# Start addresses of the SBUF buffers modulo 256 bytes in a two-layer hybrid network

## The chip, the core and the metric

The kernel runs on one core of a Trainium2 chip. The metric is the device time of one execution in microseconds, median of three runs. The core's engines appear in the profile as PE (TensorE, matrix products; PEld is its weight load), DVE (VectorE), ACT (ScalarE), POOL (GpSimd) and SP (SyncE, which only issues transfers). SBUF is the on-chip memory from which TensorE reads both operands of a product, PSUM the memory into which it writes. A product has a stationary operand (the weights, 128 by 128) and a moving one (128 rows, here 128 to 512 columns).

## The reference

Two layers over 1024 latent tokens, with 256 context tokens beside them, model width 1024. Layer 0 mixes tokens by a chunked gMLP, layer 1 by windowed attention; each is followed by a convolutional gated FFN (hidden width 2816).

```
h = modulate(rms_norm(x, norm_g[i, 0]), sh1, sc1)
layer 0:  y = chunk_mlp(h, ...)          # z = gelu(h @ w_in); u, v = split(z); v = layer_norm(v)
                                         # s = w_s (128 x 128 per group) applied to v; y = (u * s) @ w_out
layer 1:  y = window_attention(h, hc, ...)   # |q - k| <= 128 plus all context keys plus a sink
x = x + g1 * rms_norm(y, norm_g[i, 1])
h = modulate(rms_norm(x, norm_g[i, 2]), sh2, sc2)
x = x + g2 * rms_norm(conv_ffn(h, ...), norm_g[i, 3])
# conv_ffn: a, b = split(h @ w_up); a = width-3 depthwise conv of a + conv_b; (gelu(a) * b) @ w_down
```

sh, sc and g come from silu(c) @ ada_w + ada_b. All of it is float32. The context tokens go through layer 0 whole and serve layer 1 as keys and values only.

## The kernel before, in words

Each float32 operand is split into two float32r tiles, a rounded "hi" (a CAST on ACT) and a remainder "lo" (a subtraction on DVE). A product is three matmuls: hi with hi, hi with lo, lo with hi (`mm3`; two in the attention). Names in the profile read out<-moving,stationary: in the up-projection (`psB<-cmb,wh`) the inputs move and the weights stand, in the down-projection (`psA<-wh,ah`), the gMLP (`wh,big`, `wh,act`) and qkv the weights move and the activations stand.

Buffers are rings of tiles with one tag. In the pool `sb`, for the whole kernel: raw (3, float32 weights as loaded), row (10, general), wh and wl (4 each, split weights), gate, sm. In pools by stage, opened one after another at the same place by `open_pool` (mix, up0, down0, mix2, up1, down1): tmp (8), big (8, split inputs of the mixers), act (6), y, acc; in the up stages the 28 cmb tiles; in the down stages ah and al. Tiles of one ring stand one behind the other, so the address of a tile modulo 256 follows from the size of a tile and from what was laid out ahead of the ring.

Stages in order: gMLP of latent tiles 0 to 4, gMLP of latent tiles 5 to 7 and the context; 22 context jobs of the up-projection of layer 0 (256 columns, `up_ctx`); up0 (`up`, 22 jobs); down0 with the context's; qkv; attention, with its output projection (`wh,oc`) set between; up1; down1.

The up-projection (`lat_ffn`) uses seven products instead of eight, with sums of the inputs made once: `combine(g)` loads a half of 512 tokens (g = 0 or 1) from xT, the transposed input in DRAM, forms a11, a12, a22, s1, s2, s3, s4 of it and writes each, split, into its cmb tile, into the columns from g * 256. A cmb tile holds two k rows (k = 0, 1). One full job f is 7 products by 4 k by 3 = 84 matmuls of 512 columns (`up`). In layer 1, where g = 1 is late (its tokens come last out of the attention), the first five f run as plain jobs (`up_plain`) on g = 0 alone, without the seven-product scheme, 256 or 258 columns; they read the first 256 columns of both k rows of a11, a12, a22 and the row tiles A21. Their other half is made by five later half jobs ("g1", 256 columns). a11 and a12 have two extra columns in front (`off`), which in layer 1 hold the tokens of the neighbouring half.

The order on each engine comes from the tile scheduler, which works on the order of the program and on the waits between tiles. It finds them from the byte ranges that instructions touch in a tile. Some instructions are held in program order (`pins`, `keep_in_program_order`): the whole prologue on four engines, and a few norms.

Of the kernel before, what the change touches and what calls it, by code (L numbers as in the profile page):

```python
# [10 lines left out]
F32 = mybir.dt.float32  # L11
F32R = mybir.dt.float32r
AF = mybir.ActivationFunctionType
ALU = mybir.AluOpType

P = 128
D = 1024
KD = D // P
# [3 lines left out]
FFN = 2816  # L22
NF = FFN // P
# [9 lines left out]
def hybrid_kernel(  # L33
# [27 lines left out]
    sb = ctx.enter_context(tc.tile_pool(name="sb", bufs=1))  # L61
    stage_pool = {}

    def open_pool(name):
        if stage_pool:
            stage_pool.pop("guard").__exit__(None, None, None)
        stage_pool["guard"] = tc.tile_pool(name=name, bufs=1, reuse_waits="tile")
        stage_pool["pool"] = stage_pool["guard"].__enter__()

# [6 lines left out]
    def nm(s):  # L76
        uid[0] += 1
        return f"{s}_{uid[0]}"

    def t_raw():  # L80
        return sb.tile([P, 1024], F32, name=nm("raw"), tag="raw", bufs=3)

    def t_row(dt=F32, shape=(P, 1024)):
        return sb.tile(list(shape), dt, name=nm("row"), tag="row", bufs=10)

    def t_tmp(shape=(P, 648), dt=F32):
        return stage_pool["pool"].tile(list(shape), dt, name=nm("tmp"), tag="tmp", bufs=8)

    def t_big(shape, dt=F32R):
        return stage_pool["pool"].tile(list(shape), dt, name=nm("big"), tag="big", bufs=8)  # L90

    def t_act(shape=(P, 2, 644), dt=F32R):
        return stage_pool["pool"].tile(list(shape), dt, name=nm("act"), tag="act", bufs=6)

    def t_y(shape=(P, 5, 1024), dt=F32):
        return stage_pool["pool"].tile(list(shape), dt, name=nm("y"), tag="y", bufs=1)

    def t_acc():
# [5 lines left out]
    def t_sm(w=2):  # L104
        return sb.tile([P, w], F32, name=nm("sm"), tag="sm", bufs=24)

    def t_w(tag, dt=F32R, shape=(P, 1024)):
        return sb.tile(list(shape), dt, name=nm(tag), tag=tag, bufs=4)

    def psA(shape=(P, 2, 512)):  # L110
        return ps.tile(list(shape), F32, name=nm("psA"), tag="psA", bufs=2)
# [12 lines left out]
    def w_cols(w, col):  # L124
        return wsplit(w[:, col:col + P].rearrange("(k p) n -> p k n", p=P), KD)
# [27 lines left out]
    ident = const.tile([P, P], F32, name="ident")  # L153
    make_identity(nc, ident)
    ones_r = const.tile([P, P], F32R, name="ones")
    ones_f = t_tmp((P, P))
    G.memset(ones_f, 1.0)
    S.copy(ones_r, ones_f)
    ones = ones_r.bitcast(F32)
# [13 lines left out]
    def mod_cols(l, m, s):  # L173
        if (l, m) not in slots:
            slots[(l, m)] = len(slots)
        return modc[:, slots[(l, m)], s, :]
# [76 lines left out]
    def step(gen, n=1):  # L253
        for _ in range(n):
            next(gen, None)
# [51 lines left out]

    def hk(hb, z, k):
        if (z, k // 2) not in hb:
            hb[z, k // 2] = t_big((P, 2, 648))  # L310
        return hb[z, k // 2][:, k % 2, :]

    def build(hb, stage, l, mi, segs, zeros, W):
# [12 lines left out]
        for k in range(KD):  # L326
# [8 lines left out]
            S.copy(hk(hb, 0, k)[:, 0:W], tm[:, 0:W])  # L335
            V.tensor_sub(hk(hb, 1, k)[:, 0:W], tm[:, 0:W], hk(hb, 0, k)[:, 0:W])
            yield

    def halo(hb, xt, l, mi, c, col):
        tm = t_sm(KD)  # L340
        V.tensor_tensor(out=tm, in0=xt[:, :, c], in1=mod_cols(l, mi + 1, 0), op=ALU.mult)
        V.tensor_tensor(out=tm, in0=tm, in1=mod_cols(l, mi, 0), op=ALU.add)
        for q in range(KD // 2):
            V.tensor_copy(hb[0, q][:, :, col], tm[:, 2 * q:2 * q + 2])
            V.tensor_sub(hb[1, q][:, :, col], tm[:, 2 * q:2 * q + 2], hb[0, q][:, :, col])

    def up_cols(p, w, hb, c0, hw, halves=(0, 1)):
        wh, wl = w
# [80 lines left out]
    def lazy_y():  # L429
        box = []  # L430

        def y():
            if not box:
                box.append(t_y())
            return box[0]

        return y
# [281 lines left out]
    cols = {}  # L719
# [159 lines left out]
        group(3, finisher(0, tiles, y, gate, order, on_flip, mod, own), pre_last(),  # L879
              (lambda: s_part(14, True), lambda: s_part(15, True)), own)  # L880

    def ffn(l, stage, hb, W, nb, tiles, joff, gate, extra, pre_last, n_extra=1):
        hw, nbh = W // 2, 1 if nb <= 512 else 2
        bw = nb // nbh
        halves = tuple(range(nbh))
        order = list(range(len(tiles)))
        y = lazy_y()
        groups = [4, 4, 4, 4, 6]
        pend = []
        f = 0  # L890
        cw = cols["cw", l]

        def ab(f, fi, acts):
            wa = w_cols(w_up[l], f * P)
            pa = psA()
            up_cols(pa, wa, hb, 0, hw)
            wb = w_cols(w_up[l], FFN + f * P)
            pb = psA()
            up_cols(pb, wb, hb, 2, bw, halves)
            a = t_tmp()  # L900
            S.copy(a[:, 0:W].rearrange("p (a b) -> p a b", a=2), pa[:, :, 0:hw])
            cv = t_tmp()
            c = cv[:, 0:nb]
            G.tensor_scalar(out=c, in0=a[:, 2:2 + nb], scalar1=cw[:, NF + f:NF + f + 1],
                            scalar2=cols["cb", l][:, f:f + 1], op0=ALU.mult, op1=ALU.add)
            V.scalar_tensor_tensor(out=c, in0=a[:, 1:1 + nb], scalar=cw[:, f:f + 1], in1=c,
                                   op0=ALU.mult, op1=ALU.add)
            V.scalar_tensor_tensor(out=c, in0=a[:, 3:3 + nb], scalar=cw[:, 2 * NF + f:2 * NF + f + 1], in1=c,
                                   op0=ALU.mult, op1=ALU.add)
            S.activation(c, c, AF.Gelu_apprx_tanh)  # L910
            c2 = c.rearrange("p (a b) -> p a b", a=nbh)
            V.tensor_tensor(out=c2, in0=pb[:, 0:nbh, 0:bw], in1=c2, op=ALU.mult)
            if fi % 2 == 0:
                acts.append((t_act(), t_act()))
            ah, al = acts[-1]
            S.copy(ah[:, fi % 2, 0:nb], c)
            V.tensor_sub(al[:, fi % 2, 0:nb], c, ah[:, fi % 2, 0:nb])

        for gi, gn in enumerate(groups):
            acts, f0 = [], f  # L920
            for fi in range(gn):
                ab(f, fi, acts)
                f += 1
                step(extra, n_extra)
                if fi == 0 and pend:
                    pend.pop()()
            if gi < len(groups) - 1:
                pend.append(lambda f0=f0, gn=gn, acts=acts, gi=gi:
                            down_group(w_down[l], f0, gn, acts, joff, y, gi == 0, order))
        down_group(w_down[l], f0, gn, acts, joff, y, False, order,  # L930
                   finisher(stage, tiles, y, gate, order), pre_last())

    COMBOS = ("a11", "s2", "s1", "s3", "a12", "a22", "s4")

    def split_into(dst, src):
# [43 lines left out]
    def lat_ffn(l, stage, n0, halos, gate, between, steady, ctx=None, after=None):  # L979
# [2 lines left out]
        cb = cols["cb", l]  # L982
        open_pool("up%d" % l)
        pool = stage_pool["pool"]
        off = {n: 2 if n in ("a11", "a12") else 0 for n in COMBOS}
        HL = {}
        for n in COMBOS:
            for c in range(2):
                HL[n, c] = [pool.tile([P, 2, 512 + off[n]], F32R, name=nm("cmb"), tag="cmb%d_%d%s%d" % (l, z, n, c),
                                      bufs=1) for z in range(2)]  # L990
        keep = pool.tile([P, NF], F32, name=nm("keep"), tag="keep", bufs=1)

        def t_s():
# [87 lines left out]
        def up_ctx(f, nxt, fill):  # L1081
            W, more = next_weights(nxt)
            banks = [psB() for _ in range(2)]
            for bank, names in zip(banks, (("b11", "b21"), ("b12", "b22"))):
                for q in range(2):
                    for k in range(4):
                        wh, wl = (W[names[q]][z][:, k, :] for z in range(2))
                        mm3(bank[:, 0:CTX], wh, wl, cx[0, q][:, k, :], cx[1, q][:, k, :],
                            q == 0 and k == 0, q == 1 and k == 3)
                if bank is banks[0]:  # L1090
                    a = t_row(shape=(P, 1028))
                    for e in (0, 1 + CTX):
                        G.memset(a[:, e:e + 1], 0.0)
                    S.copy(a[:, 1:1 + CTX], bank[:, 0:CTX])
                step(more)
                step(fill)
            step(more, 9)
            conv_gate(f, a, CTX, banks[1][:, 0:CTX], SEQ)

        def up_plain(f, nxt, fill):  # L1100
# [3 lines left out]
            for pair_, half in ((("b11", "b21"), X), (("b12", "b22"), Y)):  # L1104
# [14 lines left out]
                    step(fill)  # L1119
                    step(more)  # L1120
                if half is X:
                    a = t_row(shape=(P, 1028))
                    G.memset(a[:, 0:1], 0.0)
                    S.copy(a[:, 1:257], X[:, 2:258])
                    S.copy(a[:, 513:514], X[:, 1:2])
                    S.copy(a[:, 257:513], X2[:, 0:256])
                    G.tensor_copy(keep[:, f:f + 1], a[:, 512:513])
# [3 lines left out]
        def up(f, groups, nxt):  # L1131
# [39 lines left out]
            product(Y, "s3", "t3", False)  # L1171
            S.copy(b2, wide(Y[:, 0:n]))
            product(X, "a12", "b21", False)
            a = t_row(shape=(P, 1028))
            av = halves(a[:, 1:1 + N])
            S.copy(av[:, :, 0, :], wide(X[:, 0:n]))
            if groups[0] == 0:
# [240 lines left out]
         flushes(True), first_weights, on_ctx, order=(3, 4, 0, 1, 2), mod=(0, 3))  # L1418

    def mix_pool():  # L1420
        open_pool("mix2")
        hold["h"] = {}
        return build(hold["h"], 2, 1, 0, [(0, 0, 640)], [], 640)

# [451 lines left out]
```

## Time and profile before

| | |
|---|---|
| median of 3 runs | 2947.26 us (2941.18 to 2949.09) |
| profiled execution, span from first to last instruction | 2937.7 us |
| instructions | 40168, of which 14834 matmuls |

The profiled execution's span lies 9.6 us below the median of the runs; sums below are made against the span.

The page lists per engine the busy time, its share of the span and the number of instructions, and the granted clock in tenths in 40 equal slices (PEclk, 9 is full). A row of the chain of waits has start, length and the work; a row of the timeline start, length of the group, engine, operands, shape of weights and moving tile, count. Durations of matmuls overlap, since a matmul's end includes the way through the array; the distance between two starts is what a matmul costs in a stream. Stages in the timeline: gMLP to about 830 us, context jobs 835 to 920, up0 to 1354, down0 to 1582, context down to 1690, qkv 1725 to 1835, attention to 2200, up1 2240 to 2685, down1 to 2938.

### The profile page before, as it was taken

The numbers are of one execution on the slowest core, as the hardware profiler recorded it, in microseconds if no ns is written. First come the engines' busy times: TensorE is split into PE (matmuls) and PEld (weight loads), VectorE is DVE, ScalarE is ACT, GpSimd is POOL, SyncE is SP. The second block draws the span as 40 slices with busy tenths as digits, with TensorE's granted clock in tenths as the row PEclk, the third lists the DMA queues.
The fourth block names the chain that finished last, engine by engine and source line by source line (L and its number), as shares of the span: only waits on it lengthen the run. The fifth ranks groups of instructions, "written<-read, shape, count | busy, mean of one in ns | idle before, by whom it ended". The sixth has DMA issues, their size and how long they took to land. (4 is left out here: it accounts for less than half of the span.)

```text
span 2937.7 us, 40168 instructions
## 1 busy us (share of the span) xinstructions
PE 2829.4 (96%) x14834; PEld 2404.4 (82%) x14834; DVE 2034.1 (69%) x3066; ACT 1353.6 (46%) x2279; POOL 678.1 (23%) x1003
## 2 busy tenths in 40 slices
PE   7999999999999999999999999899998999999999
PEld 5899988899898888888877777888887888888887
DVE  6557674756787888778643769897877877776333
ACT  4332242322575444543324534777775444444221
POOL 1151130720201212220003025564551211220000
PEclk9999999999999999999999999999999999999999
DMA  7764356532675333546844865356666233325532
GB/s 260 243 186 143 117 184 205 168 96 72 198 226 169 108 103 112 165 151 218 290 163 170 283 212 176 111 191 215 196 234 201 98 112 109 92 83 193 177 115 101
DMA packets 402310, 488.08 MB, mean 166 GB/s; under 512 B 17473, under 2 KB 296897, under 8 KB 402113
## 3 DMA queue, kind: packets, MB, share of 16 engines
q1 hardware_dynamic: 345697, 422.32, 44.7%
q10 hardware_dynamic: 55264, 58.99, 5.9%
q0 software_dynamic: 1152, 4.19, 0.4%
q8 instruction: 117, 1.92, 0.3%
q14 instruction: 80, 0.66, 0.1%
HBM read 388.96 MB, written 96.47 MB: 165 GB/s over the span
## 5 line engine op out<-in xcount | busy, mean ns | idle before, releaser
L50 PE MATMUL psB<-cmb,wh 128*128 128x512 f32 (+2 forms) x2584 | 756.5, 377 | 6.6 <-ACT s L50 3.2
L50 ACT CAST wh<-raw 128x1024 fp32r<-128x1024 f32 (+1 forms) x388 | 345.8, 904 | 510.5 <-PE psB L50 208.0
L50 PEld LDWEIGHTS psB<-cmb,wh 128*128 128x128 f32 x2584 | 471.5, 188 | 104.8 <-ACT row L50 4.4
L50 DVE TENSOR_TENSOR wl<-raw,wh 128x1024 fp32r<-128x1024 f32 (+1 forms) x388 | 399.1, 1040 | 131.4 <-ACT wh L50 130.6
L50 PE MATMUL psB<-cmb,wl 128*128 128x512 f32 (+2 forms) x1292 | 486.9, 377 | 0.0
L50 PE MATMUL psB<-wh,big 128*128 128x512 f32 x864 | 288.4, 402 | 2.7 <-DVE row L50 1.4
L50 PEld LDWEIGHTS psB<-cmb,wl 128*128 128x128 f32 x1292 | 243.1, 188 | 48.2
L50 POOL TENSOR_SCALAR sm<-sm 128x1 f32<-128x1 f32 (+1 forms) x76 | 41.4, 545 | 867.4 <-ACT tmp L50 317.2
L50 POOL TENSOR_TENSOR row<-raw,raw 128x512 f32<-128x512 f32 x44 | 72.5, 1647 | 606.4 <-DMA raw<-in_f_w_up_dram 489.4
L50 DVE TENSOR_TENSOR al<-raw,ah 128x1024 fp32r<-128x1024 f32 x74 | 90.5, 1224 | 167.8 <-ACT ah L50 167.6
L50 PE MATMUL psB<-wh,act 128*128 128x512 f32 x640 | 202.9, 395 | 1.6 <-DVE tmp L50 1.6
L50 PEld LDWEIGHTS psB<-wh,big 128*128 128x128 f32 x864 | 163.9, 191 | 42.4 <-ACT big L50 2.4
L50 PE MATMUL psA<-big,wh 128*128 128x320 f32 x1024 | 193.3, 310 | 2.6 <-ACT wh L50 1.4
L50 DVE SCALAR_TENSOR_TENSOR row<-row,cwcols,row 128x1024 f32<-128x1024 f32 (+2 forms) x142 | 160.5, 1130 | 37.9 <-ACT row L50 17.3
L50 ACT CAST ah<-raw 128x1024 fp32r<-128x1024 f32 x74 | 77.4, 1047 | 222.0 <-PE psB L50 150.6
L50 ACT CAST wh<-row 128x512 fp32r<-128x512 f32 (+1 forms) x132 | 100.7, 765 | 168.8 <-DVE row L50 77.4
L50 PE MATMUL psB<-wl,big 128*128 128x512 f32 x432 | 168.3, 399 | 0.0
L50 PEld LDWEIGHTS psA<-big,wh 128*128 128x128 f32 x1024 | 159.7, 188 | 3.6 <-ACT wh L50 2.0
L50 POOL TENSOR_SCALAR row<-row,sm,sm 128x128 f32<-128x128 f32 x160 | 120.5, 768 | 149.1 <-DMA row<-vscr 143.3
L50 PEld LDWEIGHTS psB<-wh,act 128*128 128x128 f32 x640 | 120.1, 188 | 30.1 <-issue 1.0
L50 PE MATMUL psB<-row,wh 128*128 128x256 f32 x744 | 137.1, 286 | 4.8 <-ACT wh L50 2.1
L50 DVE SCALAR_TENSOR_TENSOR acc<-raw,ccols,acc 128x1024 f32<-128x1024 f32 x63 | 79.7, 1287 | 87.1 <-DMA raw<-in_ada_w_dram 86.9
(264 smaller groups left out, 6285.6 us busy)
## 6 DMA issues: line engine op xcount, KB each, us to landing
raw<-in_f_w_up_dram SPq DMA_DIRECT2D x142, 512.0 KB, 4.4
raw<-actd SPq DMA_DIRECT2D x83, 512.0 KB, 4.3
raw<-in_a_w_in_dram SPq DMA_DIRECT2D x64, 512.0 KB, 4.6
raw<-in_ada_w_dram SPq DMA_DIRECT2D x64, 512.0 KB, 4.8
wh<-woscr SPq DMA_DIRECT2D x48, 512.0 KB, 4.3
raw<-in_f_w_down_dram SPq DMA_DIRECT2D x88, 256.0 KB, 4.0
actd<-row SPq DMA_DIRECT2D x39, 512.0 KB, 2.6
raw<-in_a_w_out_dram SPq DMA_DIRECT2D x35, 512.0 KB, 3.5
```

What stands on the lines that cost most here:

```text
L50: ins = fn(*a, **kw)
```

## The change

The pitch of every ring that TensorE reads becomes a multiple of 256 bytes, and small "lead" tiles set where a ring begins. The table gives the start modulo 256 of the tiles, as they are laid out in the two programs.

| tiles | before | after |
|---|---|---|
| raw (and oc, same ring) | 192 | 192 |
| wh, wl | 192 | 0 (lead of 16 floats) |
| row | 192, 224, 0, 32 ... (pitch 4128) | 192 (pitch 4352) |
| tmp | steps of 32 (pitch 2592) | 0 |
| big | 0, 64, 128, 192 (pitch 5184) | 0 in mix, 192 in mix2 |
| act | steps of 32 (pitch 5152) | 0 in mix, 192 in mix2 |
| cmb, first operand column | a11 0 to 96, s1 s2 s3 128, a12 128 to 224, a22 s4 0, k = 1 of a11 and a12 8 further | 0; in layer 1 the k = 1 rows of a11 and a12 at 16 |
| ah, al | 0 | 0 |

What is called distance below is the start of the stationary tile of the next matmul minus that of the moving tile of the current one, modulo 256. After the change it is, in steps between matmuls of 512 columns: 7231 times 0, 1152 times 192 (qkv, attention's output projection), 204 times 240 (steps into k = 1 of a11 and a12, layer 1). With 256 columns: 2270 times 64 (context jobs, attention), 598 times 0 (half jobs and some plain ones), 120 times 240. With 320 columns (first gMLP): 1535 times 0.

A cmb tile was [P, 2, n]; it is now a flat [P, lead + 2 pitch], of which the code takes a view with k as a dimension. In layer 0 a11 and a12 have no extra columns any more. ones_f becomes a tile of the row ring instead of tmp. Functions `halo` and `ffn`, which nothing calls, are gone.

```diff
+    leads = {"w": 16}
+    def sb_lead(tag):
+        n = leads.pop(tag, 0)
+        if n:
+            G.memset(sb.tile([P, n], F32, name=nm("lead"), tag="lead" + tag, bufs=1), 0.0)
...
+    def t_edged(n):
+        return sb.tile([P, 1088], F32, name=nm("row"), tag="row", bufs=10)[:, 0:n]
...
-    def t_tmp(shape=(P, 648), dt=F32):
+    def t_tmp(shape=(P, 640), dt=F32):
...
     def t_big(shape, dt=F32R):
+        lead("big")
...
-    def t_act(shape=(P, 2, 644), dt=F32R):
+    def t_act(shape=(P, 2, 640), dt=F32R):
+        lead("act")
...
     def t_w(tag, dt=F32R, shape=(P, 1024)):
+        sb_lead("w")
...
-    ones_f = t_tmp((P, P))
+    ones_f = t_row(shape=(P, P))
...
-            hb[z, k // 2] = t_big((P, 2, 648))
+            hb[z, k // 2] = t_big((P, 2, 640))
...
-        off = {n: 2 if n in ("a11", "a12") else 0 for n in COMBOS}
+        off = {n: 2 if n0 and n in ("a11", "a12") else 0 for n in COMBOS}
         HL = {}
+        home = 0
         for n in COMBOS:
+            pitch = 512 + 2 * off[n]
             for c in range(2):
-                HL[n, c] = [pool.tile([P, 2, 512 + off[n]], F32R, name=nm("cmb"), tag="cmb%d_%d%s%d" % (l, z, n, c),
-                                      bufs=1) for z in range(2)]
+                HL[n, c] = []
+                for z in range(2):
+                    lead_ = (-home - 4 * off[n]) % 256 // 4
+                    t = pool.tile([P, lead_ + 2 * pitch], F32R, name=nm("cmb"), tag="cmb%d_%d%s%d" % (l, z, n, c),
+                                  bufs=1)
+                    home += -(-4 * (lead_ + 2 * pitch) // 32) * 32
+                    HL[n, c].append(t[:, lead_:].rearrange("p (k n) -> p k n", k=2))
...
-            a = t_row(shape=(P, 1028))
+            a = t_edged(1028)
...
-        open_pool("mix2")
+        open_pool("mix2", big=48, y=16)
```

The order of instructions moves at two places. SP's queue begins before the change with the load of a_w_s (w_s of the gMLP):

```order
L50 DMA row_733<-in_a_w_s_dram 128x8x128
L50 DMA tmp_84<-in_c_dram 8x128
L50 DMA tmp_84<-in_c_ctx_dram 8x128
L50 DMA act_112<-in_ada_w_dram 128x4x128 x2
L50 DMA act_115<-in_ada_w_dram 128x4x128 x2
```

After the change that load stands behind the prologue's loads of w_in (raw):

```order
L50 DMA raw_412<-in_a_w_in_dram 128x2x512
L50 DMA raw_484<-in_a_w_in_dram 128x2x512
L50 DMA raw_561<-in_a_w_in_dram 128x2x512
L50 DMA row_735<-in_a_w_s_dram 128x8x128
L50 DMA row_737<-in_a_b_s_dram 128x1024
```

It moved 27 places back; the rest of the queue keeps its order there.

The second place is on PE in the plain jobs of layer 1, about 2240 us, where the last transposes out of the attention (`psA<-ident,row`) stand between the products. cmb_20599 to cmb_20602 are a11 (hi and lo, c = 0 and 1), row_20629 is A21, psB_21103 and psB_21104 the banks of the second plain job. Before, its products follow k by k, both banks in turn:

```order
L50 MATMUL psA_20923<-ident,row_20867 128x128 x7
L50 MATMUL psB_21103<-cmb_20601,wl_21002 128x258
L50 MATMUL psB_21104<-row_20629,wh_21001 128x256 x2
L50 MATMUL psB_21104<-row_20629,wl_21002 128x256
L50 MATMUL psB_21103<-cmb_20601,wh_21001 128x258
L50 MATMUL psB_21103<-cmb_20602,wh_21001 128x258
L50 MATMUL psB_21103<-cmb_20601,wl_21002 128x258
```

After the change (numbers are six higher: psB_21110 is the second bank of that job) only the products of the bank that reads A21 and the like stand there; the first products of other jobs follow, and then the k = 1 product of the first job's psA_20974 with cmb_20605 (a11, hi, c = 0), with a wait for ACT that has no counterpart before (it is for the cast by which combine(1) writes that tile):

```order
L50 MATMUL psA_21111<-row_20634,wl_21040 128x256
L50 MATMUL psB_21244<-cmb_20605,wh_21143 128x258 [waits PE_49,Activation_49]
L50 MATMUL psB_21244<-cmb_20606,wh_21143 128x258
L50 MATMUL psB_21244<-cmb_20605,wl_21144 128x258
L50 MATMUL psB_21245<-row_20634,wh_21143 128x256 [waits Activation_49]
L50 MATMUL psB_21245<-row_20634,wh_21143 128x256
L50 MATMUL psB_21245<-row_20634,wl_21144 128x256
L50 MATMUL psB_21245<-row_20634,wh_21143 128x256 x2
L50 MATMUL psA_20974<-cmb_20605,wh_20968 128x256 [waits Activation_49]
```

176 matmuls change their places around there, and with them neighbours on ACT, DVE, SP and POOL; elsewhere PE's order is that of before. Between the last transposes and the last row above stand 33 matmuls.

More of the change, by code (lines that the diff above doesn't have):

```diff
@@ L62, in hybrid_kernel, with open_pool @@
     stage_pool = {}
-    def open_pool(name):
+    def open_pool(name, **leads):
         if stage_pool:
             stage_pool.pop("guard").__exit__(None, None, None)
+        stage_pool["leads"] = leads
         stage_pool["guard"] = tc.tile_pool(name=name, bufs=1, reuse_waits="tile")
@@ L81, in t_raw, with lead @@
         return sb.tile([P, 1024], F32, name=nm("raw"), tag="raw", bufs=3)
+    leads = {"w": 16}
[3 more added lines that the diff above has]
+            G.memset(sb.tile([P, n], F32, name=nm("lead"), tag="lead" + tag, bufs=1), 0.0)
     def t_row(dt=F32, shape=(P, 1024)):
         return sb.tile(list(shape), dt, name=nm("row"), tag="row", bufs=10)
-    def t_tmp(shape=(P, 648), dt=F32):
+    def t_edged(n):
+        return sb.tile([P, 1088], F32, name=nm("row"), tag="row", bufs=10)[:, 0:n]
+    def lead(tag):
+        n = stage_pool["leads"].pop(tag, 0)
+        if n:
+            G.memset(stage_pool["pool"].tile([P, n], F32, name=nm("lead"), tag="lead" + tag, bufs=1), 0.0)
+    def t_tmp(shape=(P, 640), dt=F32):
         return stage_pool["pool"].tile(list(shape), dt, name=nm("tmp"), tag="tmp", bufs=8)
     def t_big(shape, dt=F32R):
+        lead("big")
         return stage_pool["pool"].tile(list(shape), dt, name=nm("big"), tag="big", bufs=8)
-    def t_act(shape=(P, 2, 644), dt=F32R):
+    def t_act(shape=(P, 2, 640), dt=F32R):
+        lead("act")
         return stage_pool["pool"].tile(list(shape), dt, name=nm("act"), tag="act", bufs=6)
     def t_y(shape=(P, 5, 1024), dt=F32):
+        lead("y")
         return stage_pool["pool"].tile(list(shape), dt, name=nm("y"), tag="y", bufs=1)
@@ L337, in build @@
             yield
[L339 to L345, printed above, removed]
     def up_cols(p, w, hb, c0, hw, halves=(0, 1)):
@@ L880, in gmlp @@
               (lambda: s_part(14, True), lambda: s_part(15, True)), own)
[L882 to L931, printed above, removed]
@@ L1121, in up_plain @@
                 if half is X:
-                    a = t_row(shape=(P, 1028))
+                    a = t_edged(1028)
                     G.memset(a[:, 0:1], 0.0)
@@ L1173, in up @@
             product(X, "a12", "b21", False)
-            a = t_row(shape=(P, 1028))
+            a = t_edged(1028)
             av = halves(a[:, 1:1 + N])
```

## Prediction

> **What bounds the kernel now.** I read the page first (what is busy, and at which clock), then the chain of waits in the second down-projection, then the starts of single matmuls in the timeline, since a chain row gives only the length of a block.
>
> ```profile
> span 2937.7 us, 40168 instructions
> PE 2829.4 (96%) x14834; PEld 2404.4 (82%) x14834; DVE 2034.1 (69%) x3066; ACT 1353.6 (46%) x2279; POOL 678.1 (23%) x1003
> PEclk9999999999999999999999999999999999999999
> ```
>
> TensorE is busy 96% of the span at full clock in every slice, and weight loading (82%) runs beside it. No other engine is near. So the time is the number of matmuls times their start-to-start gap, plus about 110 us of stalls, and a change of addresses can act only through the gap, or through waits that new tiles bring.
>
> The chain of waits, at the point of layer 1's down-projection where the operands change (start, length, matmuls):
>
> ```profile
> 2684.97 2.77 PE psA L50 x12
> 2687.74 2.72 PE psB L50 x12
> ...
> 2695.89 2.80 PE psA L50 x12
> 2698.69 2.80 PE psB L50 x12
> ```
>
> These are blocks of twelve 512-column matmuls, back to back, same engine, clock and precision. Up to 2695.89 the moving tiles (wh, wl) and the stationary ones (activations kept in wh/wl buffers) lie 0 apart modulo 256. After it, the stationary ones are ah/al, 64 away. The gap is 2.72/12 = 226.7 ns at distance 0 and 2.80/12 = 233.3 ns at 64: 6.6 ns, or 3%. The first block at 0 still takes 2.77, so the better gap needs about one block to settle.
>
> In layer 0's up-projection one can test whether this is the distance or the stage. Timeline rows (start, length of the group, operands):
>
> ```profile
> 1139.84 0.62 PE L50 MATMUL psB<-cmb,wh 128*128 128x512 f32 x2
> ...
> 1331.71 0.39 PE L50 MATMUL psB<-cmb,wh 128*128 128x512 f32 x1
> 1334.46 0.39 PE L50 MATMUL psB<-cmb,wh 128*128 128x512 f32 x1
> 1337.23 0.39 PE L50 MATMUL psB<-cmb,wh 128*128 128x512 f32 x1
> 1345.63 0.39 PE L50 MATMUL psB<-cmb,wh 128*128 128x512 f32 x1
> ...
> 1353.69 0.39 PE L50 MATMUL psB<-cmb,wl 128*128 128x512 f32 x1
> ```
>
> From 1331.71 to 1334.46 stand 12 matmuls at distance 192: 2.75/12 = 229.2 ns. From 1337.23 to 1345.63 stand 36 at distance 64: 8.40/36 = 233.3, the value of the other stage. Eleven whole jobs (923 intervals from 1139.84 to 1353.69), mixed in distance, average 231.7. So distance, not stage, sets the gap: 0 best, 192 next, 64 worst. No 512-column stream at 240 stands alone; I put it at 231, between 229.2 and 233.3.
>
> For 256 columns the order is another:
>
> ```profile
> 838.56 0.40 PE L50 MATMUL psB<-row,wh 128*128 128x256 f32 x2
> 863.65 0.28 PE L50 MATMUL psB<-row,wl 128*128 128x256 f32 x1
> 2001.29 1.36 PE L50 MATMUL psB<-act,y 128*128 128x256 f32 x10
> 2002.49 0.40 PE L50 MATMUL psA<-wh,oc 128*128 128x512 f32 x1
> 2356.71 0.40 PE L50 MATMUL psB<-cmb,wh 128*128 128x256 f32 x2
> 2360.81 0.40 PE L50 MATMUL psB<-cmb,wh 128*128 128x256 f32 x2
> ```
>
> The context jobs, mixed, take 25.09 us for 212 intervals, 118.3 ns. The ten of act,y at distance 0 take 1.20 us, 120 ns. The 36 of cmb at distance 64 (2356.71 to 2360.81) take 113.9. So the change picks for each width the distance that is best in this trace.
>
> **The change, part by part.** Counts are from the groups by line, operation and shape (each group with wl as stationary has half as many as its wh row; the down stage has six groups of 336):
>
> ```profile
> L50 PE MATMUL psB<-cmb,wh 128*128 128x512 f32 x2184 | 683.2, 394 | 1.7 <-DVE row L50 0.9 <-ACT row L50 0.9
> L50 PE MATMUL psA<-wh,ah 128*128 128x512 f32 x336 | 133.4, 398 | 3.3 <-DVE y L50 3.3
> L50 PE MATMUL psB<-wh,big 128*128 128x512 f32 x864 | 288.4, 402 | 2.7 <-DVE row L50 1.4 <-ACT big L50 1.3
> L50 PE MATMUL psB<-wh,act 128*128 128x512 f32 x640 | 202.9, 395 | 1.6 <-DVE tmp L50 1.6
> L50 PE MATMUL psB<-row,wh 128*128 128x256 f32 x744 | 137.1, 286 | 4.8 <-ACT wh L50 2.1 <-ACT row L50 1.5 <-DVE row L50 1.1
> L50 PE MATMUL psB<-act,y 128*128 128x256 f32 x608 | 86.7, 288 | 4.7 <-DVE sm L50 2.7 <-DVE act L50 1.2 <-DVE row L50 0.3
> ```
>
> Their mean durations (394 and so on) contain the drain of the pipe and are not the gap; only starts are used.
>
> - Up-projection, 512 columns: 2184 + 1092 = 3276 matmuls from 231.7 to 226.7, 16.4 us; less 0.9 for the 204 steps at 240 in layer 1 (204 x 4.3 ns): gain 15.5.
> - Down-projection: 6 x 336 = 2016, 64 becomes 0, 6.6 ns each: gain 13.3.
> - gMLP and qkv, rows:
>
> ```profile
> 440.80 0.39 PE L50 MATMUL psB<-wl,big 128*128 128x512 f32 x1
> 521.57 0.63 PE L50 MATMUL psB<-wh,big 128*128 128x512 f32 x2
> ...
> 1725.74 0.39 PE L50 MATMUL psB<-wl,big 128*128 128x512 f32 x1
> 1780.20 0.40 PE L50 MATMUL psA<-wl,big 128*128 128x512 f32 x1
> ```
>
> 349 intervals in 80.77 us are 231.4; 234 in 54.46 are 232.7. The gMLP's 960 with big go to 226.7 (I count 900 of them, the others stand behind waits of the start): 4.2. The 960 with act, which rotated through eight remainders, get the same 5 ns: 4.8. qkv's 624 go to distance 192: 624 x 3.5 = 2.2. Together 11.
> - Context jobs: 744 + 372 = 1116 from 118.3 to 113.9: 4.9.
> - Attention: 608 with act,y and about 384 with big,tmp go to 64, some 5 ns each, 5.0 at most. Half is taken (next fence): 2.5.
> - 480 cmb matmuls of 256 columns (the half jobs of layer 1) come to distance 0: 2.7 ns worse by my own bound (from a mixed 117 to 120): loss 1.3.
> - 1536 matmuls of 320 columns in the first gMLP come to 0, which no stream of that width shows. Bounds from the neighbours: 1.7 worse each as with 256 (loss 2.6), 5.0 better as with 512 (gain 7.7); taken 1, near the middle but towards nothing, since 320 is nearer to 256.
> - a_w_s (the first load on SP) moves behind the loads that the first matmuls need, and ones_f becomes a row tile. These are 512 KB ahead of everything; gain 0 to 1.7, taken 1. It passes SP's queue only; its user comes much later. Two lead memsets on POOL and the removed functions: nothing, POOL has 77% free and nobody waits there.
> - Settling (0.05 us on each re-entry after a break, from 2.77 against 2.72; some 60 breaks): loss 3.
> - Gains that turn into waits, where TensorE is held up by others:
>
> ```profile
> 840.00:900.00 60.00, 57.01 (x473) 55.99 (x472) 48.50 (x72) 42.48 (x71) 1.15 (x18) 1.00 0.78 230
> 1800.00:1980.00 180.00, 169.55 (x1134) 149.33 (x1133) 155.36 (x382) 129.99 (x313) 106.25 (x179) 1.00 0.45 147
> ```
>
> In these stretches (columns after the length: PE, weight load, DVE, ACT, POOL) TensorE stands still 3.0 of 60 us and 10.4 of 180, with VectorE busy 81 and 86%. A faster TensorE there waits longer: loss 4 beside the halved attention term.
>
> **A wait that the change adds.** The new cmb tiles are flat, [P, lead + 2 pitch], and k is only a view. combine(1) writes columns 256 up of both k rows of a tile that the plain jobs still read in columns 0 to 255. In the old [P, 2, n] tile the read of k=1 is a row of its own beside that write; in the flat tile it lies between the write's first and last element, and a wait for combine(1)'s cast appears on it: the order of the change shows it in the first plain job of layer 1. Rows there:
>
> ```profile
> 2241.54 1.03 PE L50 MATMUL psA<-ident,row 128*128 128x128 f32 x8
> ...
> 2249.26 0.52 ACTq L50 DMA_DIRECT2D xT<-row  x1
> ...
> 2258.57 0.62 ACT L50 CAST cmb<-row 128x512 fp32r<-128x512 f32 x1 [3.88 <-DMA row<-xT]
> ```
>
> The cast cannot come earlier: it needs the transposes at 2241.54, their eviction, the store at 2249.26 and the load back, and ends at 2259.2. TensorE did plain jobs meanwhile. In the changed order only 33 matmuls stand between those transposes and the wait, 33 x 0.118 = 3.9 us from 2242.3. What is queued behind is all of TensorE: later products and plain jobs. New idle time 2259.2 - 2242.3 - 3.9 = 13, less the 1.7 us that it waited there anyhow, less some 1.5 of waits further on that this delay swallows: loss 10 (bounds 4, if the load-back comes earlier and more products move ahead, and 13).
>
> Sum: 15.5 + 13.3 + 11 + 4.9 + 2.5 - 1.3 + 1 + 1 - 3 - 4 - 10 = 30.9, say 31. The profiled span goes from 2937.7 to about 2907. The median of the runs is 2947.3 (2941.2 to 2949.1), 9.6 above the span, so the time is about 2916. From no change a measurement can tell about 0.3%, 9 us.
>
> **A rule against it.** The Trainium skill (SBUF — State Buffer, Who interferes with whom) gives TensorE two read ports, one for the moving operand and one for the weights, independent of each other; by it no distance could matter, and the sum would hold only the waits, some 10 us slower. The trace disagrees, with 226.7 against 233.3 ns in neighbouring blocks. The page TensorE: Matmul & The Clock Gate (Back-to-back issue gap) has N/2.4 + 2.5 ns, an estimate of 215.8 for 512 columns; even the best gap here is above it.
>
> **The rivals.**
> - The wait costs nothing, because the transposes and the load-back move ahead by as much. For it: the rest of the order hardly moves. Against: the cast hangs on a DMA round trip of nearly 10 us (2249.26 to 2258.57). 31 + 10 = 41: 2906.
> - Distance 0 stays unsettled in the busy stages. For it, in attention's output projection, also at distance 0:
>
> ```profile
> 2012.70 0.63 PE L50 MATMUL psA<-wh,oc 128*128 128x512 f32 x2
> 2013.17 0.60 PE L50 MATMUL psB<-ident,row 128*128 128x128 f32 x4
> ```
>
> Two matmuls in 0.47 us, 235 each. Against: that stream is cut every few matmuls; an up job has 84 in a row. At the first block's 2.77/12 = 230.8 throughout, the up term falls from 16.4 to 2.9, the gMLP's from 9.0 to 1.6, the down-projection's from 13.3 to 5.0; of the 31 and the 3 for settling 5 remain. Halfway between 5 and 31 is 18: 2929.
> - The distance does not act as read (the difference lies in which buffer is read, not how far apart): no gain, the wait stays, 2947 to 2957. Against it are 192 and 64 inside one stage, with the same tiles.
> - Slower: distance 0 settles in the slow mode of the row above, 235, where operands come from different rings. There are 7231 such steps after the change; at 235 instead of a mean 231.9 that is +22, to 2969 before the other terms. It decides from about 232 up. Against: the one clean stream at 0 has 226.7 for three blocks of twelve, though between tiles of two rings with one start address.
> - VectorE as the new bound: no.
>
> ```profile
> L50 DVE TENSOR_TENSOR wl<-raw,wh 128x1024 fp32r<-128x1024 f32 x256 | 312.7, 1225 | 130.2 <-ACT wh L50 129.4
> L50 DVE TENSOR_TENSOR al<-raw,ah 128x1024 fp32r<-128x1024 f32 x74 | 90.5, 1224 | 167.8 <-ACT ah L50 167.6
> ```
>
> Its operands lie 0 apart in the first row and 64 in the second: 1225 and 1224 ns. Addresses move nothing there.
>
> **How the numbers follow.** The forecast (31 us, its own range 2906 to 2926) has 0.58, the free wait 0.14, the half-settled gap 0.15, no effect 0.08, the slow mode 0.05. The range 2900 to 2938 holds the first three but for their tails. Faster by over 0.3%: 0.58 + 0.14 + 0.12 = 0.84. Within 0.3%: 0.03 of the half-settled and 0.05 of no effect, 0.08. Slower: 0.03 of no effect and the slow mode, 0.08.
>
> **What would show it.** In the changed profile: blocks of twelve in both down stages at 2.72 throughout; an up0 job of 84 at 19.04 us instead of 19.46; context jobs near 114 ns; attention's windows hardly shorter; a new wait of TensorE on a cast of cmb between 2240 and 2262 of the old time axis, of some 10 us. The prediction fails if up0 keeps 231.7 at distance 0, or if that wait is far from 10.

## The result and the profile after

The changed kernel takes 2926.86 us (2924.16 to 2928.0, four runs) against 2948.18 us; the ratio is 0.9928 (95% interval 0.9913 to 0.9942), 21 us faster. The forecast was 2916, with a range of 2900 to 2938.

The page of the changed kernel, the lines that answer to those of before (span; busy time, share and count by engine; granted clock in 40 slices):

```profile
span 2925.6 us, 40176 instructions
PE 2802.7 (96%) x14834; PEld 2412.0 (82%) x14834; DVE 2028.0 (69%) x3066; ACT 1352.5 (46%) x2279; POOL 678.6 (23%) x1006
PEclk9999999999999999999999999999998999999999
```

TensorE is as busy as it was, in share; one slice of the clock, that around 2230 us, has dropped. The chain of waits at the start of the second down-projection, where the blocks went from 2.72 to 2.80 before:

```profile
2679.12 2.72 PE psA L50 x12
2681.84 2.72 PE psB L50 x12
...
2690.00 2.72 PE psA L50 x12
2692.72 2.72 PE psB L50 x12
2695.44 2.72 PE psA L50 x12
```

Now they stay at 2.72 after the operands change to ah and al (2690.00). Layer 0's up-projection, two starts ten jobs (840 matmuls) apart in the timeline:

```profile
1133.40 0.62 PE L50 MATMUL psB<-cmb,wh 128*128 128x512 f32 x2
...
1323.82 0.61 PE L50 MATMUL psB<-cmb,wh 128*128 128x512 f32 x2
```

190.42/840 = 226.7 ns, a job in 19.04 us. So the gaps came as read. What the time did not get shows when each start-to-start interval of the two traces is sorted: up to 1.3 times the median of its group it counts as gap, and what lies beyond the mean gap in a longer one is a wait. An interval is counted with the matmul that begins it; the few transposes at the very start, each of a shape of its own, are left out. The trace of before here is that of E0 below.

| moving tile, stationary tile, columns | matmuls | gap, ns | gaps, us | waits, us |
|---|---|---|---|---|
| cmb, wh/wl, 512 | 3276 | 231.7 to 227.5 | -13.7 | -2.7 |
| wh/wl, ah/al, 512 | 2015 | 233.4 to 226.8 | -13.2 | +8.4 |
| wh/wl, big, 512 | 1584 | 232.2 to 228.6 | -5.7 | +4.6 |
| wh/wl, act, 512 | 960 | 232.2 to 227.4 | -4.6 | +1.4 |
| row, wh/wl, 256 | 1176 | 118.4 to 115.9 | -3.0 | +12.7 |
| act, y, 256 | 608 | 118.9 to 115.8 | -1.9 | +0.7 |
| cmb, wh/wl, 256 | 660 | 117.0 to 119.3 | +1.5 | -0.2 |
| big, wh/wl, 320 | 1536 | 146.5 to 146.6 | +0.1 | +1.3 |
| all groups | | | -42.0 | +26.4 |

The gaps gave 42 us, and 26 of them were lost again in waits. The second profile of the changed kernel (E8) gives 44 and 29 against the same trace; and the two profiles of before differ by 4.3 us in their waits alone, so the split holds to a few us. The largest single wait that is new is the one forecast (it stands in the table's row of row, wh/wl, behind whose matmul it comes), in layer 1's plain jobs (timeline and windows; columns of a window: length, PE, weight load, DVE, ACT, POOL busy, granted clock, DMA share, GB/s):

```profile
2228.83 1.97 PE L50 MATMUL psA<-ident,row 128*128 128x128 f32 x8 [9.20 <-POOL row L50]
2237.85 0.50 PE L50 MATMUL psA<-cmb,wh 128*128 128x256 f32 x2 [3.04 <-DVE row L50]
2247.90 0.79 PE L50 MATMUL psA<-cmb,wh 128*128 128x256 f32 x2 [5.89 <-ACT cmb L50]
```
```profile
2237.00:2248.00 11.00, 4.26 (x21) 3.99 (x21) 1.09 (x4) 2.03 (x6) 0.28 (x2) 0.72 0.64 191
2248.00:2256.00 8.00, 8.00 (x52) 8.00 (x53) 7.50 (x12) 5.97 (x9) 0.00 (x0) 0.74 0.01 3
2256.00:2264.00 8.00, 8.00 (x69) 8.00 (x69) 6.32 (x8) 5.58 (x10) 1.00 (x2) 1.00 0.68 230
```

TensorE stands 5.89 us for the cast of cmb, after 3.04 for an eviction, and the granted clock is 0.72 in that window, 0.74 in the next and back at 1.00 only after 2256. The 159 matmuls behind the last transposes take 31.8 us instead of 19.75, and the next 200 take 4.1 less, since waits that stood there are covered: net 8.0.

### The profile page after: what moved, and what is told of

Read it like the earlier page. It is cut to its first block, busy times and chain, and to the rows that moved or that the text cites. A ratio compares the mean times of both kernels' runs of the same rounds, so it can differ in the third digit from the quotient of the medians.

```text
span 2925.6 us, 40176 instructions
## 1 busy us (share of the span) xinstructions
PE 2802.7 (96%) x14834; PEld 2412.0 (82%) x14834; DVE 2028.0 (69%) x3066; ACT 1352.5 (46%) x2279; POOL 678.6 (23%) x1006
## 3 DMA queue, kind: packets, MB, share of 16 engines
q0 software_dynamic: 1152, 4.19, 0.4%
## 5 line engine op out<-in xcount | busy, mean ns | idle before, releaser
L50 PE MATMUL psB<-cmb,wh 128*128 128x512 f32 (+2 forms) x2584 | 748.9, 374 | 2.4 <-ACT row L50 1.4
L50 ACT CAST wh<-row 128x512 fp32r<-128x512 f32 x132 | 100.6, 764 | 167.8 <-DVE row L50 82.4
```

The source lines that it names most:

```text
L50: ins = fn(*a, **kw)
```

## The experiments

All times are medians of their own runs; the kernel before stood at 2947.8 to 2948.6 us in each job.

**E0: before again.** No edit.

> The kernel before once more, for a second profile of it: the profile shown has a span of 2937.7, 9.6 below the median of its runs, while the changed kernel's stands 1.3 below. If the profiled execution of before was a lucky one, this one has a span of 2940 to 2950, and the difference stands in waits, not in gaps. If executions of before carry some 10 us outside the span, the span is 2936 to 2940 again.

2944.80 us, ratio to before 0.9992 (0.9980 to 1.0004), and a span of 2941.9. The gaps agree with the first profile to 0.2 us in sum; waits make 4.3. So the first profile came from a short execution, and the 9.6 us between its span and the median weren't a fixed part outside the span: E0's profiled execution took 2943.71, 1.8 more than its span, and the changed kernel's too is 1.8 above.

**E8: the changed kernel again.** No edit.

> The changed kernel once more, as the base for E1 and E9 and for a second profile. Theory (E1's gain over it is real): 2925 to 2929 again, with the wait of some 9 us on a cast of cmb near 2240 us. Rival (E1 and this differ by the scatter of the runs): 2920 to 2923.

2926.85 us, ratio 0.9928 (0.9915 to 0.9940): the same number again. The wait on the cast is 6.29 us, after 3.03.

**E3: wh and wl at 192.**

```diff
-        sb_lead("w")
-        return sb.tile(list(shape), dt, name=nm(tag), tag=tag, bufs=4)
+        t = sb.tile(list(shape), dt, name=nm(tag), tag=tag, bufs=4)
+        if tag == "wl":
+            sb_lead("w")
+        return t
```

> The changed kernel with the lead of 64 bytes behind the wh and wl rings instead of ahead of them: only these two rings move, to 192; instructions are the same. Up-projection 0 becomes 192, down-projection and gMLP 0 becomes 64, qkv 192 becomes 0, context jobs 64 becomes 0. Theory (distance sets the gap): down blocks of twelve at 2.80 us instead of 2.72 (13 us), up gaps 229.4 instead of 227.3 (6.5 us), gMLP 233 instead of 227.3 (11 us), qkv 227.5 instead of 230.2 (2 us less), 320 columns 145.2 instead of 146.6 (2 us less); about 27 us of gaps, of which up to a third disappears in waits: 2945 to 2954. Rival (what was gained came from pitches, the order or the start): within 4 us of the changed kernel, 2923 to 2931.

2948.94 us, ratio to before 1.0004 (0.9995 to 1.0013): 64 bytes of another place for two rings take back all of the gain. Chain of waits at the operand change of the second down-projection, then up0, two starts 840 matmuls apart:

```profile
2697.32 2.72 PE psA L50 x12
2700.04 2.72 PE psB L50 x12
2702.76 2.80 PE psA L50 x12
2705.56 2.80 PE psB L50 x12
```
```profile
1143.64 0.40 PE L50 MATMUL psB<-cmb,wh 128*128 128x512 f32 x1
...
1335.92 0.39 PE L50 MATMUL psB<-cmb,wh 128*128 128x512 f32 x1
```

Down at distance 64: 233.3 ns. Up at 192: 192.28/840 = 228.9. The gaps of the context jobs went to 119.8 ns, 4.6 us more, yet the groups with row as moving tile took 2.6 us less in all, since their waits fell by 7.2: a sign that TensorE doesn't pace these jobs, which E4 and E5 test. Of 31 us of worse gaps 19 reached the profile's time.

**E7: wh and wl 64 bytes on from the other rings**, the mirror of E3. Cutting rstT by 128 bytes moves every other ring back by 128 modulo 256 (cmb, ah and al from 0 to 128, row and raw from 192 to 64); wh and wl themselves start at 192, just as in E3. So only the distances are those of "wh and wl at 64".

```diff
-    leads = {"w": 16}
+    leads = {"w": 32, "v": 48}
...
+        t = sb.tile(list(shape), dt, name=nm(tag), tag=tag, bufs=4)
+        if tag == "wl":
+            sb_lead("v")
...
-    rstT = const.tile([P, 96], F32, name="rstT")
+    rstT = const.tile([P, 64], F32, name="rstT")
```

> The changed kernel with wh and wl at 64 (leads of 128 bytes ahead of and 192 behind the two rings, rstT cut by 128 bytes): up-projection at distance 64, down-projection and gMLP at 192, qkv and context jobs at 128. It mirrors E3, where the up-projection was at 192 and the down-projection at 64. Theory (distance, with its sign, sets the gap): up 233.3 instead of 227.5 (3276 matmuls, 19 us), down 229.2 instead of 226.8 (5), gMLP 229.2 (4), half jobs of 256 columns at 64 (1.6 less): 26 us of gaps, of which 20 to 26 are seen, since up0 has no waits to hide them: 2947 to 2953. Rival (only alike start addresses matter, any other distance is equally bad): up and down both near 232, 231.9 to 232.5.

2951.33 us, ratio to before 1.0009 (1.0000 to 1.0019). The same two views, in order of time:

```profile
1141.79 0.63 PE L50 MATMUL psB<-cmb,wh 128*128 128x512 f32 x2
...
1337.79 0.63 PE L50 MATMUL psB<-cmb,wh 128*128 128x512 f32 x2
```
```profile
2715.14 2.72 PE psB L50 x12
2717.86 2.75 PE psA L50 x12
2720.60 2.75 PE psB L50 x12
2723.35 2.75 PE psA L50 x12
```

Up at 64: 196.00/840 = 233.3 ns. Down at 192: 2.75/12 = 229.2. The two stages have changed places against E3, with wh and wl at the same addresses, so it is the distance, taken from the moving to the stationary operand, and neither the stage nor an unequal address as such. In the profile 32.6 us of gaps made 29.9 us of time; that execution was the longest of its ten, and by the medians it is 24.5.

**E9: every ring moved by 64 bytes, no distance between rings changed.**

```diff
     ident = const.tile([P, P], F32, name="ident")
+    G.memset(const.tile([P, 16], F32, name="shift"), 0.0)
```

> The changed kernel with a tile of 64 bytes ahead of all rings: every start address moves by 64 modulo 256, no distance changes. Theory (only the distance matters): settled gaps 226.7 ns at distance 0, 228.9 at 192, 146.7 for 320 columns, and the time of the changed kernel within 4 us. Rival (the address itself matters, such as starting at a multiple of 256): gaps of 231 to 233 in the up-projection, 13 us or more slower.

The settled gaps are those of the changed kernel: 226.7 ns at 0, 146.7 for 320 columns, and up0 takes 209.49 us for 924 matmuls in both. So the distance counts, not the address. The time is 2921.02, ratio 0.9906 (0.9893 to 0.9920), some 6 us under E8 and thus outside what was expected; the difference stands in waits (14.5 us less than in E8's profile, 9.4 of them in the groups with row as moving tile; the execution profiled was the shortest of four). Why isn't settled: E11 below doesn't separate it from scatter.

**E1: the k rows as a dimension of the tile again, with the lead in a tile of its own.**

```diff
-                    lead_ = (-home - 4 * off[n]) % 256 // 4
-                    t = pool.tile([P, lead_ + 2 * pitch], F32R, ...)
-                    home += -(-4 * (lead_ + 2 * pitch) // 32) * 32
-                    HL[n, c].append(t[:, lead_:].rearrange("p (k n) -> p k n", k=2))
+                    lead_ = (-home - 16 * off[n]) % 256 // 4
+                    if lead_:
+                        G.memset(pool.tile([P, lead_], F32, ...), 0.0)
+                    w = 512 + 4 * off[n]
+                    t = pool.tile([P, 2, w], F32R, ...)
+                    home += 4 * (lead_ + 2 * w)
+                    HL[n, c].append(t[:, :, 3 * off[n]:w])
```

> The changed kernel with one thing different: each cmb tile is again [P, 2, n] with its lead in a tile of its own, so that the k = 1 reads of the plain jobs no longer wait for combine(1)'s cast. All distances stay, but for the 204 steps at 240, which come to 224. Theory (the wait costs about what the profile shows, 12 us at its place, of which 4 are had back behind it): TensorE's idle time between the last transposes and layer 1's half-written tiles goes from about 9 us to under 3, and the time falls by 6 to 10 us, to 2917 to 2921. Rival (the loads of the up-projection set the pace anyhow and the idle time comes back a few jobs later): 2925 to 2928.

2921.74 us, ratio to before 0.9907 (0.9892 to 0.9921). Waits of TensorE in that place and a window behind it:

```profile
2232.22 1.97 PE L50 MATMUL psA<-ident,row 128*128 128x128 f32 x8 [9.20 <-POOL row L50]
2241.34 0.50 PE L50 MATMUL psA<-cmb,wh 128*128 128x256 f32 x2 [0.54 <-DVE row L50]
```
```profile
2241.50:2253.50 12.00, 12.00 (x102) 12.00 (x103) 2.77 (x3) 2.76 (x7) 0.67 (x2) 1.00 0.73 215
```

The wait on the cast is gone, the clock is full at once, and the 159 matmuls take 19.70 us as before the change. In the runs 5 us are gained, of the 6 to 10 expected; with E8's interval (0.9915 to 0.9940) beside it, the two ranges overlap a little. The 204 steps that the edit takes from 240 to 224 cost some 0.7 us of gaps.

**E2: the wait alone, at the old addresses.** a11 and a12 of layer 1 get 256 bytes of lead in a flat tile.

```diff
+                ld = 64 if n0 and off[n] else 0
-                HL[n, c] = [pool.tile([P, 2, 512 + off[n]], F32R, ...) for z in range(2)]
+                HL[n, c] = [pool.tile([P, ld + 2 * (512 + off[n])], F32R, ...)[:, ld:]
+                            .rearrange("p (k n) -> p k n", k=2) for z in range(2)]
```

> The kernel before with the wait alone: a11 and a12 of layer 1 become flat tiles with 256 bytes of lead in front, so every address modulo 256 is as before and no gap can change. Theory: 6 to 12 us slower than before (2954 to 2960), with a stall of 8 to 13 us on a cast of cmb near 2245 to 2260 us. Rival (the wait is free): within 3 us of before, 2945 to 2951.

2954.99 us, ratio to before 1.0026 (1.0016 to 1.0035): 6.4 slower, at the lower end of what was expected. The timeline has the wait:

```profile
2265.08 0.58 PE L50 MATMUL psA<-cmb,wh 128*128 128x256 f32 x1 [6.88 <-ACT cmb L50]
```

The 159 matmuls take 31.86 us, the next 200 take 4.2 less, as in the changed kernel.

**E4 and E5: half of the context jobs' loads left out**, in the kernel before and in the changed one.

```diff
-        wa, wb = t_raw(), t_raw()
-        for w, col in ((wa, f * P), (wb, FFN + f * P)):
+        half = l == 0 and plain
+        wa = t_raw()
+        wb = wa if half else t_raw()
+        for w, col in ((wa, f * P), (wb, FFN + f * P))[:1 if half else 2]:
```

> The kernel before, with half of the weights' loads left out in the context jobs (the second load of 512 KB of each job is not made, its casts and products use the first one's tile; the numbers that come out are of no meaning there). Only the context jobs and the tiles split for them carry the test, about 835 to 925 us. Theory (loads pace the context jobs): the stretch from matmul 4395 to 5090 takes about 2 to 4 us less than the 90.0 and 90.2 us of the two profiles of before. Rival (products pace it): within 1 us.

> The changed kernel, with the same half of the loads left out. Theory (loads pace the context jobs, so the better gap of 115.9 against 118.4 ns could not show): the same stretch takes 84 to 87 us instead of 93.7, and lies 2 to 4 us below that of the kernel before with half the loads, as 1116 matmuls by 2.5 ns make 2.8. Rival (something other than loads holds it, such as ACT's queue): above 90 us, and no shorter than that of before with half the loads.

The window from 835 to 920 us in four kernels: before (E0), E4, changed, E5.

```profile
835.00:920.00 85.00, 81.14 (x663) 80.11 (x662) 68.80 (x102) 60.85 (x101) 1.78 (x28) 0.98 0.77 224
```
```profile
835.00:920.00 85.00, 85.00 (x717) 84.87 (x716) 75.54 (x113) 64.53 (x110) 4.32 (x30) 1.00 0.48 145
```
```profile
835.00:920.00 85.00, 81.31 (x657) 80.66 (x656) 69.18 (x102) 58.10 (x97) 3.63 (x28) 0.94 0.75 220
```
```profile
835.00:920.00 85.00, 85.00 (x700) 84.01 (x699) 74.08 (x112) 61.86 (x106) 5.27 (x31) 1.00 0.48 148
```

With all loads TensorE stands still for 3.9 and 3.7 us of the 85; with half of them not at all. The 704 intervals from matmul 4396 on take 90.1 (E0) and 93.5 us with all, 83.3 and 82.9 with half; the whole kernels took 2941.06 (ratio 0.9971, 0.9958 to 0.9985) and 2921.18 (0.9904, 0.9885 to 0.9924). So the loads pace this stretch, as the theory says, and by more than it said (6.8 us where 2 to 4 were expected, and a stretch below the 84 to 87). Its second half failed: the changed kernel should have been 2 to 4 us ahead with half the loads, and is 0.4 ahead, for its gap was 117.3 ns there and not 113.9.

The 93.5 us are those of one execution. In E8's profile of the same kernel the stretch takes 89.7, and the gap of the row group is 114.3 ns. The windows from 880 to 895 us of the two:

```profile
880.00:895.00 15.00, 12.07 (x88) 11.67 (x87) 10.45 (x15) 10.50 (x20) 0.26 (x4) 0.84 0.76 236
```
```profile
880.00:895.00 15.00, 12.66 (x109) 12.26 (x109) 9.19 (x14) 9.46 (x17) 0.25 (x4) 1.00 0.76 232
```

TensorE stands still for 2.9 and 2.3 us, but in the first the granted clock is 0.84 as well, and 88 matmuls stand where E8 has 109. What the better gap is worth in this stretch is less than what its executions differ by. The timeline of the changed kernel shows why the gap is not 113.9 throughout (starts of two stretches, 207 and 171 matmuls):

```profile
839.60 0.40 PE L50 MATMUL psB<-row,wh 128*128 128x256 f32 x2
...
863.98 0.40 PE L50 MATMUL psB<-row,wh 128*128 128x256 f32 x2
...
866.98 0.39 PE L50 MATMUL psB<-row,wh 128*128 128x256 f32 x2
...
886.36 0.39 PE L50 MATMUL psB<-row,wh 128*128 128x256 f32 x2
```

24.38/207 = 117.8 ns, then, same operands and distance, 19.38/171 = 113.3. Between them, at about 865.6, lie two steps of some 0.2 us. At distance 64 a stream of 256 columns has two speeds and keeps the one that it got at its last break: in E5 840 intervals in a row ran at 117.8.

**E6: E1 with a third buffer for the loads of ada_w** beside the first down-projection.

```diff
-                            lambda: pool.tile([P, 1024], F32, name=nm("araw"), tag="araw", bufs=2))
+                            lambda: pool.tile([P, 1024], F32, name=nm("araw"), tag="araw", bufs=3))
```

The reason, in the changed kernel's timeline, VectorE and TensorE in the middle of that stage:

```profile
1453.41 1.28 DVE L50 SCALAR_TENSOR_TENSOR dacc<-araw,ccols,dacc 128x1024 f32<-128x1024 f32 x1 [2.35 <-DMA araw<-in_ada_w_dram]
1458.82 0.75 DVE L50 TENSOR_SCALAR dacc<-araw,ccols 128x1024 f32<-128x1024 f32 x1 [4.12 <-DMA araw<-in_ada_w_dram]
...
1460.62 0.69 DVE L50 TENSOR_TENSOR y<-psA,gate 128x512 f32<-128x512 f32 x1
...
1461.36 0.79 PE L50 MATMUL psA<-wh,ah 128*128 128x512 f32 x1 [6.37 <-DVE y L50]
```

The eviction that frees the bank (y out of psA) stands in VectorE's queue behind sums that wait for loads. In the first profile of before the same wait was 3.28, in E0's 0.79. A likely reading, not shown, is that the wait depends on how early TensorE comes to loads that it doesn't speed up.

> The kernel with separate k rows (E1) with a third buffer for the loads of ada_w that run beside the first down-projection (ring araw). Theory (in the middle of that stage TensorE waits for VectorE's eviction, which stands in VectorE's queue behind sums that wait for these loads, 2.4 and 4.1 us): the wait on DVE y near 1461 us falls from 6.4 to about 3, and the time by 2 to 4 us against E1's 2921.7. Rival (the transfers themselves are too slow, more buffers only move the wait): within 1.5 us of E1.

2917.83 us, ratio to before 0.9887 (0.9868 to 0.9906).

```profile
1459.18 0.79 PE L50 MATMUL psA<-wh,ah 128*128 128x512 f32 x1 [5.28 <-DVE y L50]
```

The wait went from E1's 6.73 to 5.28, not to 3; but E8 has 5.29 without the buffer, and E10 and E11, with the same third buffer, have 2.33 and 0.40. So it differs as much between executions as the edit was to change it. The 3.9 us against E1 lie within overlapping intervals; that the buffer brings them isn't shown.

**E10: E6 with the load of a_w_s early.**

```diff
     S.copy(ones_r, ones_f)
+    aws = t_row()
+    Q.dma_start(aws.rearrange("p (g q) -> p g q", g=8), w_s[0].rearrange("g p q -> p g q"))
...
-        wt = t_row()
-        Q.dma_start(wt.rearrange("p (g q) -> p g q", g=8), w_s[0].rearrange("g p q -> p g q"))
+        wt = aws
```

> E6 (separate k rows, third araw buffer) with the load of a_w_s back at the head of SP's queue, second there. Theory (in its new place those 512 KB delay the loads of conv_w by their own length, hence the new wait of 1.6 us on DVE cwcols at 98 us): that wait goes, TensorE's first matmul comes 1.5 to 2.3 us later, and the time is that of E6, 2917.8, within 2. Rival (the wait at 98 us comes from TensorE's faster gMLP, not from the load): the wait stays and the later start is lost, 1.5 to 2.5 us slower.

2918.47 us, ratio to before 0.9892 (0.9877 to 0.9907). The changed kernel's wait and E10's:

```profile
98.11 0.50 PE L50 MATMUL psA<-wh,big 128*128 128x512 f32 x1 [1.62 <-DVE cwcols L50]
```
```profile
96.72 0.50 PE L50 MATMUL psA<-wh,big 128*128 128x512 f32 x1 [0.77 <-DVE cwcols L50]
```

E6, which E10 differs from by this edit, has 1.71 there. But E8 and E11 have 0.95 and 0.91 without the edit, so it isn't shown that the edit halves the wait; and against the theory the wait doesn't go. The first matmul starts 2.4 us later (6.66 against 4.29). In the time it is nothing, as expected.

**E11: E6 with E9's shift**, both edits as above.

> E6 (separate k rows, third araw buffer) with E9's shift of all rings by 64 bytes. E9 was some 6 us faster than the changed kernel with the same gaps, the difference in waits for loads. Theory (the shift does something to the loads): 2910 to 2913. Rival (E9's 6 us came from which waits its executions happened on, the shift does nothing): 2915 to 2920, as E6's 2917.8. The settled gaps are 226.7 at distance 0 in both.

2910.87 us in the median, ratio to before 0.9882 (0.9863 to 0.9900). That is the theory's number, but E6's interval, 0.9868 to 0.9906, covers most of it: the shift's effect stays open. The context stretch, short in E9 (86.8 us for the 704 intervals), takes 90.4 here with the same shift, so that part of E9's lead did not come back. This is the fastest version run.

## Why the prediction was right, step by step

- **Distance sets the gap, 0 best for 512 columns.** Right, and shown from three sides: the changed kernel (up 226.7 at 0, down 226.7 at 0), E3 (up 228.9 at 192, down 233.3 at 64), E7 (up 233.3 at 64, down 229 at 192), with the order of instructions alike and E9 excluding the address itself. The three values forecast for them, 226.7, 229.2 and 233.3, were read off the trace of before.
- **Up-projection, 15.5:** 13.7. The average is 227.5, not 226.7, since each stream starts slowly (first twelve 229.0 ns on average). Down-projection, 13.3: 13.2. gMLP and qkv, 11: 10.3. Settling, 3: the 7231 steps at 0 average 227.3 ns, which is some 4 us above 226.7. Half jobs, -1.3: -1.5.
- **The Trainium skill's independent ports (SBUF — State Buffer, Who interferes with whom):** by them no distance matters; in E3 the down-projection goes from 226.7 to 233.3 ns, 3%, with only two rings moved.
- **Context jobs, 4.9:** the gap gave 3.0 in the first profile and 4.8 in E8's, and the stretch took 93.5 and 89.7 us after 90.1 before, so nothing of it is seen in the time. Two errors: the stretch is paced by loads (E4, E5), and 113.9 was one of two speeds (113.3 and 117.8). The forecast saw 3.0 us of idle time in 60 there, and took it as a small discount instead of as the sign of another bound.
- **Attention, 2.5:** the gaps of its 256-column products gave 2.2; its 2493 matmuls took 393.3 and 397.3 us in the two profiles of before and 395.6 and 396.4 in those after, hardly shorter, as was said.
- **320 columns:** taken 1 better, is 0.1 worse, within the bounds.
- **The added wait, 10 (4 to 13):** 8.0 net in the profile, 6.4 by E2 alone, 5 by taking it away (E1). TensorE's idle time there is 3.0 and 5.9 us, less than the 13 that the forecast started from. Its cause was told wrong: not flatness but the lead inside the flat tile brings it. Built flat without a lead, the program has PE's order of before; that program was not run.
- **Gains that turn into waits, 4:** this is the term that was mis-sized. Waits grew by 26.4 us in all against E0, and by 28.7 in E8's profile; without the 8 of the cast about 18 and 21. 8.0 of the 26.4 lie in the first down-projection (E6's place among them), which the forecast priced like the second one, whose blocks stand without a wait: the last 1059 matmuls, the second one, went from 247.2 to 240.8 us, 944 of the first one from 225.1 and 221.5 to 223.3 and 222.4. The term is no fixed number: E9, with gaps like those of the changed kernel, has 14.2.
- **Start, +1:** the first matmul came 2.4 us earlier than in E0, and the end of the first 600 matmuls 0.9 us later, in E8's profile 0.4 earlier.

Sum by the profiles: 42 - 26 = 16 between E0 and the changed kernel, 21 between the medians of the runs, 31 forecast. The gaps were right to 2 us (44 forecast after settling); the waits were forecast at 14.

The measured 2926.86 lies just beyond the forecast's own range (2906 to 2926) and nearer to the 2929 of the rival with the half-settled gap. That rival is not what happened: behind the first twelve matmuls of a stream, all 449 whole blocks of twelve at distance 0 lie within 0.5 ns of 226.7 in the changed kernel. The mechanism came as told, and it was mainly the waits that took the other 10 us. The rivals with no gain or with a slow mode at 0 fall by the same blocks, and the free wait falls by E2.

## What to carry to other kernels

Where TensorE is busy 96% of the time, sort the start-to-start intervals of its matmuls by the distance of the two operands' start addresses modulo 256 bytes before anything else: 226.7 against 233.3 ns could be read in neighbouring blocks of one trace, and in E3 64 bytes in the place of two rings decided the whole gain. Price such a gain stage by stage. Here it came in full where TensorE never waited, as in the second down-projection; where loads set the pace, as in the context jobs, it came back as a wait. A tile that is given a lead and then viewed as rows can lose the tracking of its rows: look for new waits in the order, and keep the lead in a tile of its own.

## What the runs showed of the hardware that was not expected

- A stream of 256-column matmuls at distance 64 runs at 113.3 or at 117.8 ns, from one break to the next, up to 840 intervals long; which one changes from run to run. 512 columns at 0 have one speed in the changed kernel, once the first twelve of a stream are past: the 449 blocks above, within 0.5 ns of 226.7.
- Two waits of 3.0 and 5.9 us, close behind a 9.2 us one, went with a granted clock of 0.72, and the first 8 us after them held 52 matmuls where the next 8 held 69: by an estimate from these counts some 2 us of the wait's price are the clock's. In E1, where 0.54 us stand in their place, the 12 us behind had the clock at 1.00.
- Moving every ring by 64 bytes with all distances kept left the gaps alone and yet took some 6 us off the time, in waits; the runs here don't say whether that is more than chance.
